# Two projection groups side by side at the start of a hybrid decoder block, and one set of copies moved to ScalarE

## The chip, the cores and the metric

The kernel runs on one core of a Trainium2 chip. Its metric is the device time of one execution in microseconds. A core has five engines with an instruction queue each: TensorE (PE, with its weight loads as PEld) multiplies matrices into PSUM banks; VectorE (DVE), ScalarE (ACT) and GpSimd (POOL) do elementwise work; SyncE (SP) mostly issues DMAs. An engine takes its own instructions in program order, and waits at one until the semaphores of the tiles it reads and writes allow it.

## What is computed

S = 512 positions, D = 1024, one layer, float32:

```python
h = rms_norm(x, norm_g)
proj = h @ w_in            # 4 x 512 + 4 x 512 + 2 x 1024 + 8 columns
fq, fk, fv, fz, mq, mk, mv, mz, ga, gb, fl = split_cols(proj, IN_SPLITS)
q, k = rms_norm(heads(fq)), rms_norm(heads(fk))        # 8 heads of 64
log_f = log_sigmoid(fl + b_f)
y_fox = attention(q, k, heads(fv), bias=cumsum(log_f)) * silu(fz)
q, k = rope(rms_norm(heads(mq))), rope(rms_norm(heads(mk)))
y_moba = block_attention(q, k, heads(mv)) * silu(mz)
merged = (sigmoid(ga + b_gate[0]) * (y_fox @ w_fox)
          + sigmoid(gb + b_gate[1]) * (y_moba @ w_moba))
out = x + merged @ w_out
```

## The kernel before, in words

**Products.** Every float32 operand of a projection is split in two parts of a shorter type, a high part (a rounded copy) and a low part (the rest). A product Z·w is then three matmuls: Zh·wh, Zh·wl, Zl·wh. Activations stand transposed, 1024 rows in KT = 8 slices k of 128, 512 positions each. The projection's columns are worked off in groups of 256: fqa, fka, fza, fzb, fva, then fqb, fkb, fvb, the eight m groups, wf0 to wf3 (the product with w_fox), the gate groups GA and GB, wm and wo. A group of the q, k or v kind has four units, one for each 128 positions, 24 matmuls into one PSUM bank each. A z group and a wf group have two units, transposed (L402, L403), of 512 columns.

**Weights.** A weight group arrives as one or two raw tiles of 128 x 4 x 256 (tag "wr", four buffers); `split` (L131 to L137) has ScalarE copy it to wh (L134) and VectorE subtract to get wl. `pump` issues loads ahead as buffers come free.

**The normalisation.** The first four groups do not wait for the RMS norm. `split_x` (L121 to L126) makes Zh, Zl from the raw rows of x times the norm's gain (ScalarE's product L125, VectorE's subtraction L126), and fqa, fka, fza, fzb multiply these; the factor 1/rms comes in later. `x_stats` (L218 to L229) loads x once more, in eight tiles, has ScalarE square and sum each (L225), and VectorE and GpSimd make mm and r of the sums (from L226). `norm_row` (L234 to L238) spreads r over the partitions (p_rbc, rbc), and `normalise` (L240 to L244) makes the normalised Gh and Gl, eight slices, which fva and all later groups use.

**The start.** `first_loads` (L65 to L86) issues the DMAs of the rows xt0 to xt7 and of fqa's weights on SyncE's queue, the first four slices in small pieces (k=0, k=1, k=2 and 3), the constants cs on ScalarE's queue. TensorE first runs WARM = 8 matmuls on zeros (L107). `first_split` (L148 to L160) splits fqa's weights piece by piece, with the split of the rows between; then wfl (the eight forget columns) and fka's two raw tiles are loaded whole, in `load_fl` (L139 to L146, tag "qk"). `first_qk` (L371 to L382) multiplies fqa, all eight k for its four banks, and after it fka, 264 columns wide because it carries the forget columns. fqa has its banks in "pj" and "lg", fka its in "tp" and "pv". Then come, in the program: x_stats, the evacuation of the eight banks (`evac_qk`: ScalarE's copy qn L310, for fka VectorE's xf; `norm_qk` per pair of banks: ScalarE's square L324, VectorE's reduction, GpSimd's power L331 and product L333), `forget_exp` (L444), `norm_row`, fza and fzb with `normalise` between, `forget` (L452 to L490: a chain of small VectorE operations on fg, pre, then p_c and p_LR on TensorE, c4), and fva, whose `evac_v` (L335 to L341) has a copy by ScalarE and a subtraction by VectorE (L341).

**The wf products.** `unit_f` (L680 to L691) multiplies a unit of wf into a "pj" bank and has VectorE copy it to FS (L690). The units of wf0 to wf2 run among the last attention group's steps, those of wf3 after it; mzb, just ahead, uses the same banks (evacuated at L422).

**What sets the order.** The program text gives dependences and buffers; a scheduler then orders the instructions of every engine with a timeline of its own, and this order is fixed when the kernel is built. Buffers: "pj" two PSUM banks, "lg" two, "tp" three, "pv" one; raw weights four, wh and wl four each, "qk" four, "y" (rows of x and many others) fifteen. The main sequence stands in L909 to L983.

Of the kernel before, what the change touches and what calls it, by code (L numbers as in the profile page):

```python
# [19 lines left out]
CW = 256  # L20
EPS = 1e-6
NEG = -3.0e38
WARM = 8
WR = 4

C_NG, C_BG, C_FQ, C_FK, C_MQ, C_MK, C_BF, C_GQ, C_GK, C_END = 0, 8, 24, 25, 26, 27, 28, 36, 52, 68
# [3 lines left out]
def fox_moba_kernel(ctx: ExitStack, tc, xT, x, w_in, w_fl, w_fox, w_moba, w_out, cst, rope, out):  # L30


    nc = tc.nc
    V, A, G, T = nc.vector, nc.scalar, nc.gpsimd, nc.tensor

    con = ctx.enter_context(tc.tile_pool(name="con", bufs=1))
    sb = ctx.enter_context(tc.tile_pool(name="sb", bufs=1))
# [3 lines left out]
    stage = {}  # L41
# [7 lines left out]
    def t2(tag, bufs, name, shape=(P, 512), dt=F32):  # L49
        pool = stage["pool"] if tag in ("qs", "pt", "pc", "ys") else sb  # L50
        return pool.tile(list(shape), dt, name=name, tag=tag, bufs=bufs)

    def pst(tag, bufs, name):
        return ps.tile([P, 512], F32, name=name, tag=tag, bufs=bufs)

    def pj(name):
        return pst("pj", 2, name)
# [2 lines left out]
        return pst("tp", 3, name)  # L60


    XT, RAW = {}, {}

    def first_loads():  # L65
        def xt(eng, k):
            XT[k] = t2("y", 15, f"xt{k}")
            eng.dma_start(out=XT[k], in_=xT[:, k, :])

        def w(k0, k1):  # L70
            hf = k0 // 4
            if hf not in RAW:
                RAW[hf] = sb.tile([P, 4, CW], F32, name=f"wr_fqa{hf}", tag="wr", bufs=WR)
            nc.sync.dma_start(out=RAW[hf][:, k0 - 4 * hf:k1 - 4 * hf], in_=w_in[0, :, k0:k1, :])
        nc.scalar.dma_start(out=cs, in_=cst)
        w(0, 1)
        xt(nc.sync, 0)
        w(1, 2)
        xt(nc.sync, 1)
        w(2, 4)  # L80
        xt(nc.sync, 2)
        xt(nc.sync, 3)
        w(4, 8)
        for k in range(4, KT):
            xt(nc.sync, k)


    cs = con.tile([P, C_END], F32, name="cs")
# [1 line left out]
    wfl = con.tile([P, KT, 8], F32, name="wfl")  # L90
    def col(c, n=1):
        return cs[:, c:c + n]
# [12 lines left out]
    wps = pst("tp", 3, "warm_ps")  # L105
    for i in range(WARM):
        T.matmul(wps, warm[:, :P], warm, start=True, stop=True)  # L107
# [10 lines left out]
    Gl = con.tile([P, KT, S], F32R, name="Gl")  # L118
    Z = {}

    def split_x(*ks):  # L121
        for k in ks:
            xt = XT[k]
            zh, zl = Z[k] = [stage["pool"].tile([P, S], F32R, name=f"Z{hl}{k}") for hl in "hl"]
            A.activation(zh, xt, AF.Copy, scale=col(C_NG + k))  # L125
            V.scalar_tensor_tensor(zl, xt, col(C_NG + k), zh.bitcast(F32), op0=OP.mult, op1=OP.subtract)  # L126


    chunks = {}

    def split(src, n, name, half=False):  # L131
        hi = sb.tile([P, 4, 264], F32R, name=f"wh_{name}", tag="wh", bufs=4)
        lo = sb.tile([P, 4, 264], F32R, name=f"wl_{name}", tag="wl", bufs=4)
        A.activation(hi[:, :, 0:n], src, AF.Copy)  # L134
# [4 lines left out]
    def load_fl(name, c0, hf):  # L139
        raw = sb.tile([P, 4, CW], F32, name=f"wr_{name}{hf}", tag="qk", bufs=4)  # L140
        nc.sync.dma_start(out=raw, in_=w_in[c0 // CW, :, 4 * hf:4 * hf + 4, :])
        hi, lo = split(raw, CW, f"{name}{hf}")
        f = wfl[:, 4 * hf:4 * hf + 4, :]
        A.activation(hi[:, :, CW:264], f, AF.Copy)
        V.tensor_tensor(out=lo[:, :, CW:264], in0=f, in1=hi[:, :, CW:264].bitcast(F32), op=OP.subtract)
        chunks.setdefault(name, []).append((hi, lo))  # L146

    def first_split(hf, between):  # L148
        raw = RAW[hf]
        hi = sb.tile([P, 4, 264], F32R, name=f"wh_fqa{hf}", tag="wh", bufs=4)  # L150
        lo = sb.tile([P, 4, 264], F32R, name=f"wl_fqa{hf}", tag="wl", bufs=4)
        for q, xs in enumerate(between):
            k = slice(2 * q, 2 * q + 2) if hf else slice(max(q, 2 * q - 2), max(q + 1, 2 * q))
            if hf == 0 and q < 2:
                V.tensor_copy(hi[:, k, :CW], raw[:, k])
            else:
                A.activation(hi[:, k, :CW], raw[:, k], AF.Copy)
            V.tensor_tensor(out=lo[:, k, :CW], in0=raw[:, k], in1=hi[:, k, :CW].bitcast(F32), op=OP.subtract)
            split_x(*xs)
        chunks.setdefault("fqa", []).append((hi, lo))  # L160

    COLS = {}
    off = 0
    for nm in ("fq", "fk", "fv", "fz", "mq", "mk", "mv", "mz"):
        for hfn in ("a", "b"):
            COLS[nm + hfn] = off
            off += CW
    for nm in ("ga", "gb"):
        for i in range(4):
            COLS[f"{nm}{i}"] = off  # L170
            off += CW

# [45 lines left out]
    def x_stats():  # L218
        G.memset(mh, -0.5)
        for t in range(NT):  # L220
            for hf in range(2):
                xt = t2("y", 15, f"x{t}{hf}")
                nc.sync.dma_start(out=xt, in_=x[t * P:(t + 1) * P, hf * 512:(hf + 1) * 512])
                j = t2("u", 4, "junk")
                A.activation(j, xt, AF.Square, accum_out=ms2[:, t, hf:hf + 1])  # L225
        V.tensor_add(mm, ms2[:, :, 0], ms2[:, :, 1])  # L226
        V.tensor_scalar(mm, mm, 1.0 / D, EPS, op0=OP.mult, op1=OP.add)
        V.tensor_scalar(e2, mm, EPS, None, op0=OP.mult)
        G.tensor_tensor(out=r, in0=mm, in1=mh[:, :NT], op=OP.pow)  # L229
# [138 lines left out]
                        in1=tab[:, ts, None, 24:32].to_broadcast([P, 2, 4, 8]), op=OP.mult)  # L368
        G.tensor_tensor(out=qn[:, :, :, 0:16], in0=ra, in1=rb, op=OP.add)

    def first_qk(name, tags):  # L371
        banks = [pst(tg, n, f"{name}_{i}") for i, (tg, n) in enumerate(tags)]
        n = 264 if name == "fka" else CW
        for kk in range(KT):
            hi, lo = chunks[name][kk // 4]
            k = kk % 4
            for t in range(NT):
                st = slice(t * P, (t + 1) * P)
                T.matmul(banks[t][:, :n], Z[kk][0][:, st], hi[:, k, :n], start=(kk == 0), stop=False)
                T.matmul(banks[t][:, :n], Z[kk][0][:, st], lo[:, k, :n], start=False, stop=False)  # L380
                T.matmul(banks[t][:, :n], Z[kk][1][:, st], hi[:, k, :n], start=False, stop=(kk == KT - 1))
        return banks  # L382

    def unit(name, t):
        def go():
# [283 lines left out]
    FS, MG = {}, {}  # L669

    def br_mm(p, name, br, c):
        hi, lo = chunks[name][0]
        cc = slice(c * P, (c + 1) * P)
        for k in range(4):
            yh, yl = Y[br, k]
            T.matmul(p, hi[:, k, cc], yh, start=(k == 0), stop=False)  # L676
            T.matmul(p, hi[:, k, cc], yl, start=False, stop=False)  # L677
            T.matmul(p, lo[:, k, cc], yh, start=False, stop=(k == 3))  # L678

    def unit_f(i, c):  # L680
        def go():
            j = 2 * i + c
            p = pj(f"pf{j}")
            br_mm(p, f"wf{i}", "f", c)
            if j == 0:
                f = sb.tile([P, 4, S], F32, name="f03", tag="v", bufs=2)
                FS[0], FS[1] = f[:, 0:2, :], f[:, 2:4, :]
            elif j in (4, 6):
                FS[j // 2] = sb.tile([P, 2, S], F32, name=f"f{j}", tag="qk", bufs=4)
            V.tensor_copy(FS[i][:, c, :], p)  # L690
        return go  # L691

    SG = {}
# [9 lines left out]
    def group(name):  # L703
# [213 lines left out]
    for t in range(NT):  # L917
        evac_qk(b1[t], "fqa", t)
# [5 lines left out]
    fz = filler(["fza", "fzb"])  # L924
# [119 lines left out]
```

## Time and profile before

| | |
|---|---|
| median of 3 runs | 433.29 us (433.22 to 433.48) |
| the profiled execution | 432.65 us |
| its span, first to last instruction | 430.9 us |
| instructions | 8095 |
| granted TensorE clock, mean | 1.00 |
| GpSimd's busy time | 86.6 us (20%) |
| moved by DMA | 56.13 MB, 130 GB/s on the mean |
| moved in the first 10.8 us, in the next two such slices | 245, 398, 293 GB/s |

Times of the trace are microseconds from the span's start. A row of the timeline has a start, a duration from first to last instruction of the row, the engine, the line, the operation, what is written and read, the shape, the count, and in brackets how long the engine stood idle before it and what ended that. SPq is SyncE's queue of DMA issues. A row of the groups has the count, the shortest, median and longest duration in ns, and the times of the first and the last.

### The profile page before, as it was taken

Reading aid. Unit: us, or ns where it says so; the run is one execution under the profiler, and the core shown is the slowest. Engines: PE = TensorE matmul, PEld = TensorE weight load, DVE = VectorE, ACT = ScalarE, POOL = GpSimd, SP = SyncE. Lnnn points to the kernel's source line nnn. Section 1 sums busy time; section 2 is a strip of 40 time slices with the busy share of each in tenths; the row PEclk is TensorE's granted clock in tenths of the full one; section 3 lists DMA queues with packets and bytes.
Section 4 is the critical chain, followed back from the end, with each engine's and each line's share of the span. In section 5 each row is a group of like instructions: output and inputs, shape, how many; then the busy total and the mean of one; then the engine's idle time right before and its main releaser. Section 6 shows DMA issues by size and latency. Waiting matters only on the chain.

```text
span 430.9 us, 8095 instructions
## 1 busy us (share of the span) xinstructions
PE 424.5 (99%) x3103; PEld 400.5 (93%) x3103; DVE 313.7 (73%) x559; ACT 249.6 (58%) x480; POOL 86.6 (20%) x108
## 2 busy tenths in 40 slices
PE   8999999999999999999999999999999999999996
PEld 6998899999999998999998878899999989999996
DVE  5679965869979867767856898959897796673311
ACT  4986336876868767677765855547655545531100
POOL 1049200227044660044630003020000000000000
PEclk9999999999999999999999999999999999999999
DMA  7981235326565413303304305561415306525221
GB/s 245 398 293 54 94 102 152 98 79 206 170 213 176 140 39 119 122 13 122 111 15 137 110 13 186 181 196 52 146 50 184 110 3 211 187 96 166 85 92 46
DMA packets 25670, 56.13 MB, mean 130 GB/s; under 512 B 3240, under 2 KB 11872, under 8 KB 25632
## 3 DMA queue, kind: packets, MB, share of 16 engines
q1 hardware_dynamic: 14528, 40.08, 28.0%
q10 hardware_dynamic: 9952, 11.34, 8.8%
q0 software_dynamic: 1152, 4.19, 2.7%
q8 instruction: 24, 0.39, 0.4%
q14 instruction: 14, 0.11, 0.1%
HBM read 46.01 MB, written 6.32 MB: 121 GB/s over the span
## 4 chain that ended last, share of the span: by engine, by line
PE 96%; DVE 2%; DMA 1%; issue 0%; SPq 0%; DVEq 0%
PE pb_GB L750 3%; PE pb_GA L750 3%; PE pb_GB L749 3%; PE pb_GA L747 3%; PE pb_GB L747 3%; PE pb_GA L749 3%; PE po L847 3%; PE po L849 3%; PE po L848 3%; PE pv L608 2%; PE pv L607 2%; PE lg L553 2%; PE lg L552 2%; PE pm L676 2%; PE pm L677 2%; PE pm L678 2%
## 5 line engine op out<-in xcount | busy, mean ns | idle before, releaser
L557 ACT ACTIVATE p<-p,negm 128x128 f32<-128x128 f32 (+1 forms) x64 | 35.7, 558 | 14.4 <-DVE negm L555 12.2
L331 POOL TENSOR_TENSOR ff<-ss,mh 128x8 f32<-128x8 f32 x16 | 27.8, 1743 | 65.5 <-DVE ss L329 65.1
L555 DVE CUSTOM_DVE_ANT_0 p<-lg,mask 128x128 f32<-128x128 f32 (+1 forms) x64 | 30.8, 485 | 13.0 <-PE lg L553 12.3
L847 PE MATMUL po<-wh_wo,mgh 128*128 128x256 f32 x96 | 27.1, 282 | 0.0
L849 PE MATMUL po<-wh_wo,mgl 128*128 128x256 f32 x96 | 27.0, 282 | 0.0
L848 PE MATMUL po<-wl_wo,mgh 128*128 128x256 f32 x96 | 26.9, 281 | 0.0
L857 DVE TENSOR_TENSOR ot<-po,xr 128x256 f32<-128x256 f32 x16 | 6.6, 424 | 24.7 <-PE po L849 23.5
L134 ACT ACTIVATE wh_wo<-wr_wo 128x1024 fp32r<-128x1024 f32 x8 | 8.5, 1061 | 21.6 <-PE po L849 8.0
L552 PE MATMUL lg<-KH,QS 128*128 128x128 f32 (+1 forms) x64 | 20.5, 329 | 0.0
L633 DVE TENSOR_TENSOR ypair<-pv,ysh 64x512 f32<-64x512 f32 x16 | 11.0, 687 | 12.9 <-ACT ysh L632 12.8
L136 DVE TENSOR_TENSOR wl_GB<-wr_gb,wh_GB 128x1024 fp32r<-128x1024 f32 x14 | 16.8, 1224 | 4.2 <-ACT wh_GB L134 3.3
L136 DVE TENSOR_TENSOR wl_GA<-wr_ga,wh_GA 128x1024 fp32r<-128x1024 f32 x14 | 17.9, 1294 | 2.5 <-ACT wh_GA L134 2.4
L134 ACT ACTIVATE wh_GB<-wr_gb 128x1024 fp32r<-128x1024 f32 x14 | 14.6, 1059 | 8.6 <-PE pm L677 2.5
L134 ACT ACTIVATE wh_GA<-wr_ga 128x1024 fp32r<-128x1024 f32 x14 | 14.6, 1059 | 8.5 <-PE pb_GA L749 4.3
L848 PEld LDWEIGHTS po<-wl_wo,mgh 128*128 128x128 f32 x96 | 18.1, 189 | 0.0
L849 PEld LDWEIGHTS po<-wh_wo,mgl 128*128 128x128 f32 x96 | 18.1, 189 | 0.0
L847 PEld LDWEIGHTS po<-wh_wo,mgh 128*128 128x128 f32 x96 | 18.1, 189 | 0.0
L136 DVE TENSOR_TENSOR wl_wo<-wr_wo,wh_wo 128x1024 fp32r<-128x1024 f32 x8 | 9.8, 1222 | 7.4 <-ACT wh_wo L134 7.4
L632 ACT ACTIVATE ysh<-pv 64x512 f32<-64x512 f32 x16 | 9.5, 594 | 8.9 <-PE pv L608 6.4
L604 DVE TENSOR_TENSOR ptl<-p_a,pth 128x512 fp32r<-128x512 f32 x16 | 11.0, 686 | 4.1 <-ACT pth L603 4.1
L676 PE MATMUL pf<-yhf,wh_wf 128*128 128x512 f32 x32 | 13.2, 414 | 0.6 <-DVE zs_mzb L422 0.6
L526 DVE SCALAR_TENSOR_TENSOR QS<-p_qT,cs,QS 64x512 fp32r<-64x512 f32 x16 | 12.0, 750 | 2.5 <-ACT QS L525 2.2
(447 smaller groups left out, 1769.9 us busy)
## 6 DMA issues: line engine op xcount, KB each, us to landing
wr_ga<-in_w_in_dram SPq DMA_DIRECT2D x8, 512.0 KB, 3.5
wr_gb<-in_w_in_dram SPq DMA_DIRECT2D x8, 512.0 KB, 5.0
wr_wo<-in_w_out_dram SPq DMA_DIRECT2D x8, 512.0 KB, 4.2
xt<-in_xT_dram SPq DMA_DIRECT2D x8, 256.0 KB
x<-in_x_dram SPq DMA_DIRECT2D x8, 256.0 KB, 7.2
KH<-KH ACTq DMA_DIRECT2D x16, 128.0 KB, 2.4
s_dramh<-sum_sh ACTq DMA_DIRECT2D x8, 256.0 KB
s_draml<-sum_sl ACTq DMA_DIRECT2D x8, 256.0 KB, 4.4
```

Source lines behind the costliest of these rows:

```text
L134: A.activation(hi[:, :, 0:n], src, AF.Copy)
L136: eng.tensor_tensor(out=lo[:, q, 0:n], in0=src[:, q], in1=hi[:, q, 0:n].bitcast(F32), op=OP.subtract)
L331: G.tensor_tensor(out=f2, in0=ss.rearrange("p t h -> p (t h)"), in1=mh, op=OP.pow)
L552: T.matmul(lg[:, :n], qs[:, qt], kh[:, :n], start=True, stop=False)
L555: V.tensor_tensor_reduce(pt, lg[:, :n], mask[:, 512 - n:512], -0.125, 3.0e38, op0=OP.add, op1=OP.min, accum_out=mkn[:, hh, i:i + 1])
L557: A.activation(pt, pt, AF.Exp, bias=mkn[:, hh, i:i + 1], scale=-1.0, accum_out=rs[:, hh, i:i + 1])
L747: T.matmul(o, hi[:, k, cc], lh, start=(n < 3 and c == 0 and k == 0), stop=False, skip_group_check=True)
L749: T.matmul(o, hi[:, k, cc], ll, start=False, stop=False, skip_group_check=True)
L750: T.matmul(o, lo[:, k, cc], lh, start=False, stop=(k == 3), skip_group_check=True)
L847: T.matmul(p[:, :CW], gh[:, st], hi[:, k, :CW], start=(kk == 0), stop=False)
L848: T.matmul(p[:, :CW], gh[:, st], lo[:, k, :CW], start=False, stop=False)
L849: T.matmul(p[:, :CW], gl[:, st], hi[:, k, :CW], start=False, stop=(kk == KT - 1))
```

## The change

Two parts. **The start:** fqa and fka are multiplied side by side, slice by slice: for each k first fqa's twelve products, then fka's. For that fka's weights are loaded in the same small pieces as fqa's, between the rows of x, and the first rows xt0 come in two halves of 256 positions, each split by itself. wfl goes to ScalarE's queue, right behind cs, and its split to the first use of each half of fka. Only the first piece of weights is rounded by VectorE (before, the first two). WARM is 6. `load_fl` goes; `COLS` only moves up. **The wf products:** ScalarE, not VectorE, copies the eight banks out.

```diff
-WARM = 8
+WARM = 6
...
     def first_loads():
-        def xt(eng, k):
-            XT[k] = t2("y", 15, f"xt{k}")
-            eng.dma_start(out=XT[k], in_=xT[:, k, :])
-
-        def w(k0, k1):
+        def w(nm, k0, k1):
             hf = k0 // 4
...
+            if (nm, hf) not in RAW:
+                tag, bufs = ("wr", WR) if nm == "fqa" else ("qk", 4)
+                RAW[nm, hf] = sb.tile([P, 4, CW], F32, name=f"wr_{nm}{hf}", tag=tag, bufs=bufs)
+            nc.sync.dma_start(out=RAW[nm, hf][:, k0 - 4 * hf:k1 - 4 * hf],
+                              in_=w_in[0 if nm == "fqa" else COLS["fka"] // CW, :, k0:k1, :])
+
+        def xt(k, c0=0, c1=S):
+            if k not in XT:
+                XT[k] = t2("y", 15, f"xt{k}")
+            nc.sync.dma_start(out=XT[k][:, c0:c1], in_=xT[:, k, c0:c1])
         nc.scalar.dma_start(out=cs, in_=cst)
-        w(0, 1)
-        xt(nc.sync, 0)
-        w(1, 2)
-        xt(nc.sync, 1)
-        w(2, 4)
-        xt(nc.sync, 2)
-        xt(nc.sync, 3)
-        w(4, 8)
-        for k in range(4, KT):
-            xt(nc.sync, k)
+        nc.scalar.dma_start(out=wfl, in_=w_fl)
+        w("fqa", 0, 1)
+        xt(0, 0, 256)
+        xt(0, 256, S)
+        w("fka", 0, 1)
+        w("fqa", 1, 2)
+        xt(1)
+        w("fka", 1, 2)
+        w("fqa", 2, 4)
+        xt(2)
+        w("fka", 2, 4)
+        xt(3)
+        w("fqa", 4, 8)
+        xt(4)
+        w("fka", 4, 8)
+        for k in range(5, KT):
+            xt(k)
...
-    def split_x(*ks):
...
+    def split_x(k, parts=1):
+        xt = XT[k]
+        Z[k] = [stage["pool"].tile([P, S], F32R, name=f"Z{hl}{k}") for hl in "hl"]
+        n = S // parts
+        for c in (slice(i * n, (i + 1) * n) for i in range(parts)):
+            zh, zl = (z[:, c] for z in Z[k])
+            A.activation(zh, xt[:, c], AF.Copy, scale=col(C_NG + k))
+            V.scalar_tensor_tensor(zl, xt[:, c], col(C_NG + k), zh.bitcast(F32), op0=OP.mult, op1=OP.subtract)
...
+    def first_split(nm, k0, k1, on_v=False):
+        hf = k0 // 4
+        if len(chunks.setdefault(nm, [])) == hf:
+            hi = sb.tile([P, 4, 264], F32R, name=f"wh_{nm}{hf}", tag="wh", bufs=4)
+            lo = sb.tile([P, 4, 264], F32R, name=f"wl_{nm}{hf}", tag="wl", bufs=4)
+            chunks[nm].append((hi, lo))
+            if nm == "fka":
+                f = wfl[:, 4 * hf:4 * hf + 4, :]
+                A.activation(hi[:, :, CW:264], f, AF.Copy)
+                V.tensor_tensor(out=lo[:, :, CW:264], in0=f, in1=hi[:, :, CW:264].bitcast(F32), op=OP.subtract)
+        hi, lo = chunks[nm][hf]
+        k = slice(k0 - 4 * hf, k1 - 4 * hf)
+        raw = RAW[nm, hf]
+        if on_v:
+            V.tensor_copy(hi[:, k, :CW], raw[:, k])
+        else:
+            A.activation(hi[:, k, :CW], raw[:, k], AF.Copy)
+        V.tensor_tensor(out=lo[:, k, :CW], in0=raw[:, k], in1=hi[:, k, :CW].bitcast(F32), op=OP.subtract)
...
-    def first_qk(name, tags):
...
+    def first_qk(banks, kk):
+        for name, bank in banks.items():
+            n = 264 if name == "fka" else CW
...
             for t in range(NT):
...
-            V.tensor_copy(FS[i][:, c, :], p)
+            A.activation(FS[i][:, c, :], p, AF.Copy)
...
-    first_split(0, ((0,), (1, 2), (3, 4)))
-    first_split(1, ((5, 6), (7,)))
-    nc.sync.dma_start(out=wfl, in_=w_fl)
-    load_fl("fka", COLS["fka"], 0)
-    load_fl("fka", COLS["fka"], 1)
-    b1 = first_qk("fqa", (("pj", 2), ("pj", 2), ("lg", 2), ("lg", 2)))
-    b2 = first_qk("fka", (("tp", 3), ("tp", 3), ("tp", 3), ("pv", 1)))
+    banks = {nm: [pst(tg, n, f"{nm}_{i}") for i, (tg, n) in enumerate(tags)] for nm, tags in
+             (("fqa", (("pj", 2), ("pj", 2), ("lg", 2), ("lg", 2))), ("fka", (("tp", 3), ("tp", 3), ("tp", 3), ("pv", 1))))}
+    for k0, k1 in ((0, 1), (1, 2), (2, 4), (4, 8)):
+        first_split("fqa", k0, k1, k0 == 0)
+        for k in range(k0, k1):
+            split_x(k, 2 if k == 0 else 1)
+            if k == k0:
+                first_split("fka", k0, k1)
+            first_qk(banks, k)
+    b1, b2 = banks["fqa"], banks["fka"]
     x_stats()
```

More of the change, by code (lines that the diff above doesn't have):

```diff
@@ L60, in tp @@
         return pst("tp", 3, name)
+    COLS = {}
+    off = 0
+    for nm in ("fq", "fk", "fv", "fz", "mq", "mk", "mv", "mz"):
+        for hfn in ("a", "b"):
+            COLS[nm + hfn] = off
+            off += CW
+    for nm in ("ga", "gb"):
+        for i in range(4):
+            COLS[f"{nm}{i}"] = off
+            off += CW
     XT, RAW = {}, {}
     def first_loads():
-        def xt(eng, k):
-            XT[k] = t2("y", 15, f"xt{k}")
-            eng.dma_start(out=XT[k], in_=xT[:, k, :])
-        def w(k0, k1):
+        def w(nm, k0, k1):
             hf = k0 // 4
-            if hf not in RAW:
-                RAW[hf] = sb.tile([P, 4, CW], F32, name=f"wr_fqa{hf}", tag="wr", bufs=WR)
-            nc.sync.dma_start(out=RAW[hf][:, k0 - 4 * hf:k1 - 4 * hf], in_=w_in[0, :, k0:k1, :])
-        nc.scalar.dma_start(out=cs, in_=cst)
-        w(0, 1)
-        xt(nc.sync, 0)
-        w(1, 2)
-        xt(nc.sync, 1)
-        w(2, 4)
-        xt(nc.sync, 2)
-        xt(nc.sync, 3)
-        w(4, 8)
-        for k in range(4, KT):
-            xt(nc.sync, k)
+            if (nm, hf) not in RAW:
[7 more added lines that the diff above has]
+            nc.sync.dma_start(out=XT[k][:, c0:c1], in_=xT[:, k, c0:c1])
+        nc.scalar.dma_start(out=cs, in_=cst)
+        nc.scalar.dma_start(out=wfl, in_=w_fl)
[15 more added lines that the diff above has]
+            xt(k)
     cs = con.tile([P, C_END], F32, name="cs")
@@ L119, in fox_moba_kernel @@
     Z = {}
-    def split_x(*ks):
[L122 to L126, printed above, removed]
+    def split_x(k, parts=1):
[6 more added lines that the diff above has]
+            V.scalar_tensor_tensor(zl, xt[:, c], col(C_NG + k), zh.bitcast(F32), op0=OP.mult, op1=OP.subtract)
     chunks = {}
@@ L137, in split @@
         return hi, lo
[L139 to L171, printed above, removed]
+    def first_split(nm, k0, k1, on_v=False):
[16 more added lines that the diff above has]
+        V.tensor_tensor(out=lo[:, k, :CW], in0=raw[:, k], in1=hi[:, k, :CW].bitcast(F32), op=OP.subtract)
@@ L369, in do_rope @@
         G.tensor_tensor(out=qn[:, :, :, 0:16], in0=ra, in1=rb, op=OP.add)
-    def first_qk(name, tags):
-        banks = [pst(tg, n, f"{name}_{i}") for i, (tg, n) in enumerate(tags)]
-        n = 264 if name == "fka" else CW
-        for kk in range(KT):
+    def first_qk(banks, kk):
+        for name, bank in banks.items():
+            n = 264 if name == "fka" else CW
             hi, lo = chunks[name][kk // 4]
@@ L378, in first_qk @@
                 st = slice(t * P, (t + 1) * P)
[L379 to L382, printed above, removed]
+                T.matmul(bank[t][:, :n], Z[kk][0][:, st], hi[:, k, :n], start=(kk == 0), stop=False)
+                T.matmul(bank[t][:, :n], Z[kk][0][:, st], lo[:, k, :n], start=False, stop=False)
+                T.matmul(bank[t][:, :n], Z[kk][1][:, st], hi[:, k, :n], start=False, stop=(kk == KT - 1))
     def unit(name, t):
```

## The prediction

> **What bounds the kernel now.** I began with the engines' busy shares and the chain of work that ended last.
>
> ```profile
> PE 424.5 (99%) x3103; PEld 400.5 (93%) x3103; DVE 313.7 (73%) x559; ACT 249.6 (58%) x480; POOL 86.6 (20%) x108
> PE 96%; DVE 2%; DMA 1%; issue 0%; SPq 0%; DVEq 0%
> ```
>
> TensorE is busy for 424.5 of 430.9 us and carries 96% of the chain. An edit can win only where TensorE now idles, and it loses wherever TensorE has to wait for something new. So the next view is busy time by stretch (after the times: the stretch's length, then PE, PEld, DVE, ACT, POOL).
>
> ```profile
> 0.00:5.27 5.27, 3.72 (x8) 2.51 (x8) 1.28 (x5) 2.21 (x3) 1.70 (x10) 1.00 0.56 136
> 5.27:12.27 7.00, 6.62 (x50) 5.98 (x49) 5.40 (x9) 4.57 (x8) 0.00 (x0) 1.00 1.01 362
> 28.70:54.00 25.30, 25.30 (x124) 20.96 (x124) 25.04 (x49) 14.21 (x26) 16.65 (x17) 1.00 0.30 99
> 54.00:100.00 46.00, 45.98 (x381) 45.33 (x380) 33.00 (x79) 30.14 (x67) 8.46 (x6) 1.00 0.36 107
> ```
>
> Two things stand here. Real projection work begins at 5.27 us and has small holes until 12.27, while DMA is saturated. And from 28.7 to 54, where the first groups are evacuated and normalised, **VectorE is full too**: 25.04 of 25.30 us. The change acts on the first, and I ask what it does to the second.
>
> The timeline of TensorE gives the anchors: warm-up, first product, last of fqa and first of fka, first of fza.
>
> ```profile
> 1.55 3.78 PE L107 MATMUL warm_ps<-warm 128*128 128x512 f32 x8 [1.55 <-DVE fg_pre L468]
> 5.27 0.39 PE L379 MATMUL fqa<-wh_fqa,Zh 128*128 128x256 f32 x1
> 17.92 0.28 PE L381 MATMUL fqa<-wh_fqa,Zl 128*128 128x256 f32 x1
> 18.04 0.53 PE L379 MATMUL fka<-wh_fka,Zh 128*128 128x264 f32 x3
> 29.73 0.39 PE L402 MATMUL pz_fza<-Zh,wh_fza 128*128 128x512 f32 x1
> 29.96 0.39 PE L403 MATMUL pz_fza<-Zl,wh_fza 128*128 128x512 f32 x1
> ```
>
> The 96 products of fka run without a hole: 11.69 us, 0.122 each. 17.69 to 18.04 shows fqa's dense pitch, about 0.117; 96 of these are 11.2, but fqa takes 12.77. **1.5 us of holes is all that side-by-side work can fill**, beside an earlier first product.
>
> **The change, part by part. The first stage.** The loads set its pace; these are the first users of each piece.
>
> ```profile
> 0.80 0.38 SPq L74 DMA_DIRECT2D wr_fqa<-in_w_in_dram  x1
> 1.24 0.41 SPq L68 DMA_DIRECT2D xt<-in_xT_dram  x1
> 2.17 0.43 SPq L68 DMA_DIRECT2D xt<-in_xT_dram  x1
> 3.52 0.30 DVE L155 CAST wh_fqa<-wr_fqa 128x256 fp32r<-128x256 f32 x1 [2.01 <-DMA wr_fqa<-in_w_in_dram]
> 4.50 0.72 ACT L125 ACTIVATE Zh<-xt,cs 128x512 fp32r<-128x512 f32 x1 [1.75 <-DMA xt<-in_xT_dram]
> 5.39 0.29 DVE L155 CAST wh_fqa<-wr_fqa 128x256 fp32r<-128x256 f32 x1 [1.12 <-DMA wr_fqa<-in_w_in_dram]
> 6.80 0.72 ACT L125 ACTIVATE Zh<-xt,cs 128x512 fp32r<-128x512 f32 x1 [1.58 <-DMA xt<-in_xT_dram]
> ```
>
> *First product.* A 128 KB piece of weights took 2.72 us from issue to use (0.80 to 3.52), a 256 KB one 3.26. The half piece of xt0 is issued at 1.24, so it is there between 3.96 and 4.50; I take 4.15. Its half-width split costs between 0.29 (the 128x256 cast) and 0.72; I take 0.42. First product at 4.6, bounds 4.3 to 5.0. The six warm-up products end by 1.55 + 6 x 0.43 (3.78 us for eight, less the tail of the last) = 4.1, so they don't block it.
>
> *Step k=0.* 12 x 0.117 + 12 x 0.122 = 2.87 us. Those before about 5.3 run at the warm-up's pace (0.43 for 512 columns against 0.23 at 29.73): some four of them, 0.1 each, so 0.4. TensorE could start k=1 at 4.6 + 2.87 + 0.4 = 7.9.
>
> *Step k=1* needs xt1, now the sixth SP issue and not the fourth. Counted in bytes (896 KB against 768 KB) it lands 0.5 us after the 6.80 of before, at 7.3. Counted in pieces it is later: before, landings followed each other by 0.98, 0.89 and 1.41 us, and the 128 KB piece took as long as its larger neighbour; five steps of about 1.0 after 3.52 give 8.5. I take 7.65, between them. With its 0.72 split and a handoff, k=1 starts at 8.4. Afterwards a step asks for 512 KB in 2.87 us, half of the 362 GB/s above, so nothing else waits. wfl's issue, now second on ScalarE's queue, holds up only the table load (0.4 us, done long before 4.15).
>
> The end of fka, E, is 8.4 + 7 x 2.87 = **28.5 instead of 29.73: 1.2 us early**. Bounds 27.9 (7.9 holds) and 29.4 (by pieces).
>
> **What waits behind it.** Before, fqa's banks were copied out under fka's products. Now fqa ends 12 products before fka does, and ScalarE takes its work in program order. The changed program's order there is: four qn_fqa copies, the split of fzb's first half, two qn_fka copies, and only then the square of the last x tile, from which all of VectorE's chain hangs (mm, r, rbc, the normalisation). Before:
>
> ```profile
> 25.36 1.06 ACT L134 ACTIVATE wh_fzb<-wr_fzb 128x1024 fp32r<-128x1024 f32 x1 [0.24 <-DMA wr_fzb<-in_w_in_dram]
> 27.46 0.63 ACT L225 ACTIVATE junk<-x 128x512 f32<-128x512 f32 x1 [1.03 <-DMA x<-in_x_dram]
> 29.13 1.19 ACT L310 ACTIVATE qn_fka<-fka 128x256 f32<-128x256 f32 x4
> 30.21 1.05 ACT L134 ACTIVATE wh_fzb<-wr_fzb 128x1024 fp32r<-128x1024 f32 x1
> 31.16 1.14 ACT L324 ACTIVATE sq<-qn_fka 128x512 f32<-128x512 f32 x2
> 28.21 0.16 DVE L226 TENSOR_TENSOR mm<-ms 128x4 f32<-128x4 f32 x1 [0.53 <-ACT junk L225]
> ```
>
> There the square starts as its tile lands, 27.46, and VectorE's chain at 28.21, 0.75 later. In the changed kernel fqa's last product ends at E - 12 x 0.122 - 0.117 + 0.28 = E - 1.3. Then, on ScalarE: one copy 0.33, the fzb split 0.95 (30.21 to 31.16), two copies 0.60, the square and handoff 0.75. The chain starts at **E + 1.35 = 29.85, 1.6 us later than before**, though TensorE is earlier.
>
> Its end is VectorE's evacuation of the first fva bank, for which the third fva unit (pj, two banks) waits.
>
> ```profile
> 43.69 0.18 DVE L463 SCALAR_TENSOR_TENSOR fg<-fg,fg 128x32 f32<-128x32 f32 x1
> 57.10 0.11 DVE L481 MEMSET c<- 128x64 f32 x1
> 57.84 0.42 DVE L341 TENSOR_TENSOR v_fva<-pj_fva,v_fva 128x256 fp32r<-128x256 f32 x1
> 58.01 0.28 PE L305 MATMUL pj_fva<-wh_fva,Gl 128*128 128x256 f32 x1
> 58.31 0.39 PE L303 MATMUL pj_fva<-wh_fva,Gh 128*128 128x256 f32 x1
> ```
>
> Before, it ends at 58.26 and TensorE goes on at 58.31, 0.18 later than its pitch from 58.01 asks: the two were level. From 28.21 to 58.31 are 30.1 us, and VectorE is full all the way. The changed order has the same instructions in between, less what stood from 57.10 to 57.84 (0.74) and one more fg step (0.1), plus a wait of about 0.15 for the exp that now follows the reduces: 29.4. So the third fva unit starts at E + 1.35 + 29.4 = E + 30.75 = 59.25, **0.95 us later than 58.31**. TensorE by itself would be there at E + 28.4 (from fza's start to the end of the second fva unit before, 29.73 to 58.13): it stalls 2.3 us. The early gain is spent and more.
>
> After that VectorE has slack (33.0 of 46 us from 54 to 100), and TensorE's order is that of before from the group mqb on, so I carry 0.95 to the end.
>
> **The wf products.** Eight copies go from VectorE to ScalarE.
>
> ```profile
> L690 DVE COPY f<-pf x8: 669/682/692, 249.1 to 278.6; 128x512 f32<-128x512 f32 x8
> 35.27 0.60 ACT L238 ACTIVATE rbc<-p_rbc 128x512 f32<-128x512 f32 x1 [2.85 <-PE p_rbc L237]
> 250.00:260.00 10.00, 10.00 (x51) 8.25 (x50) 9.39 (x18) 4.83 (x13) 0.00 (x0) 1.00 0.11 31
> PE pf L676 <- DVE zs_mzb L422: 0.6, 2, 0.4
> ```
>
> VectorE loses 8 x 0.68 = 5.4 us where it is nearly full, ScalarE gets 8 x 0.60 where it is half idle. But TensorE has no hole from 250 to 260; the 0.6 us it waits for pf's bank is for mzb's evacuation, which stands ahead of the first copy in both orders. Bounds: gain 0.6, loss 0.6 (one copy in front of a KH split). I take 0.
>
> **Sum.** -1.2 at fka's end, +2.15 given back at the third fva unit, 0 for wf: +0.95. The profiled execution took 432.65 us (span 430.9), 0.64 below the median 433.29; I put the difference on the median: **434.3 us**, with E's bounds 433.7 to 435.2.
>
> **Rivals.** *The clock is released late (slower).* Before, the quick pitch set in only after a burst without a pause from 1.55 to 5.27; the granted clock reads 1.00 throughout and doesn't show it, the pitch does. With six warm-ups TensorE pauses from 4.1 to 4.6. If another such spell (3.7 us) counts from 4.6, products run at about 0.215 until 8.3: 17 of the 24, the rest ends at 9.15, E is 29.25 and the time 435.0. Against it: the pause is short.
> [...]
>
> *VectorE's chain does not bind (faster).* Three rows of that chain are long:
>
> ```profile
> 34.24 0.83 DVE L459 TENSOR_TENSOR fg<-fg,fg 128x32 f32<-128x32 f32 x1
> 35.11 0.97 DVE L460 TENSOR_TENSOR fg<-fg 128x32 f32<-128x32 f32 x1
> 33.98 2.04 POOL L333 TENSOR_TENSOR qn_fqa<-qn_fqa,ff 128x512 f32<-128x512 f32 x2
> L242 DVE SCALAR_TENSOR_TENSOR xt<-xt,cs,rbc x8: 740/747/1536, 36.8 to 43.0; 128x512 f32<-128x512 f32 x8
> ```
>
> Their neighbours of that size take 0.18, and one normalisation 1.54 against 0.75; GpSimd's products run beside the first two. If GpSimd's work moves off them, 0.65 + 0.8 + 0.8 = 2.25 us goes, the stall with it, and TensorE keeps its 1.2 to 1.5: 431.9. It decides from 2.3 us on. Against: GpSimd's work hangs from the same start, so I expect it to move along.
>
> *Even.* The chain comes out 0.6 to 1 us shorter than my sum (handoffs, two of the three long rows): 433.3.
>
> **How the numbers follow.** Forecast 0.50; late clock 0.12; chain not binding 0.20; even 0.18. A difference of 0.2% (0.87 us) is about what a measurement of this kernel tells from none. Below 432.4 lies the unbound chain: 0.20. Within 0.2% lie the even case and the lower third of the forecast: 0.35. Above 434.2 lies the rest: 0.45. The range takes in most of the unbound chain's case and leaves out some 0.05 below and 0.1 above (half of the late clock, and E at its upper bound): 431.7 to 435.4.
>
> **What would show it.** First product near 4.6; xt1's split between 7.3 and 8.5; fza near 28.5; the square of the last x tile 1.3 us after its tile could have been squared, with VectorE's mm near 29.85; and a hole of about 2 us in TensorE ahead of the third fva unit, whose releaser is VectorE's v_fva. No such hole, or a quick pitch only from 8 us on, would prove me wrong.

## The result, and the profile after

| | before | after |
|---|---|---|
| median | 433.25 us (6 runs, 432.73 to 433.48) | 437.28 us (6 runs, 435.81 to 438.42) |
| ratio, 95% interval | | 1.0094, 1.0081 to 1.0106 |
| the profiled execution, its span | 432.65, 430.9 us | 435.81, 434.1 us |
| last product of TensorE ends | 427.26 us | 430.18 us |

The changed kernel is 4.0 us slower. The forecast was 434.3 in a range of 431.7 to 435.4: the sign was right, the size was not.

I read the changed kernel in the same order. Busy time by stretch (times, length, then PE, PEld, DVE, ACT, POOL, clock, DMA share, GB/s):

```profile
5.27:12.27 7.00, 7.00 (x52) 6.88 (x52) 4.41 (x10) 3.73 (x8) 0.00 (x0) 1.00 0.91 291
28.70:54.00 25.30, 25.30 (x124) 20.98 (x124) 24.36 (x48) 16.13 (x28) 17.52 (x20) 1.00 0.34 118
54.00:100.00 46.00, 44.38 (x368) 43.71 (x367) 32.74 (x78) 26.17 (x58) 5.36 (x4) 1.00 0.35 106
100.00:150.00 50.00, 48.35 (x393) 47.14 (x392) 44.98 (x93) 37.09 (x81) 25.03 (x19) 1.00 0.56 169
```

The side-by-side stage does fill its holes: TensorE is busy for 7.00 of 7.00 us where it was for 6.62. But only 52 products fall into this stretch in place of 50, since its first 1.9 us run at about half the pitch (0.21 us from one product to the next, 6.71 to 6.92, where 8.01 to 8.13 is 0.12; see the clock, below). And 1.6 us are lost between 54 and 100, and **1.65 us between 100 and 150, where the kernel before was full** (50.00). The list of TensorE's waits (what it waited for, total, times, longest) names them:

```profile
PE pj_fva L312 <- DVE v_fva L350: 1.6, 1, 1.6
PE lg L559 <- DMA KH<-KH: 0.8, 1, 0.8
PE pj_mqa L312 <- DVE v_fvb L350: 0.8, 1, 0.8
PE pf L683 <- DVE zs_mzb L429: 0.4, 1, 0.4
```

The timeline of the same kernel, the rows that answer to the steps of the forecast:

```profile
4.83 0.58 PE L387 MATMUL fqa<-wh_fqa,Zh 128*128 128x256 f32 x1 [0.36 <-ACT Zh L148]
6.71 0.41 PE L387 MATMUL fqa<-wh_fqa,Zh 128*128 128x256 f32 x1
6.92 0.41 PE L388 MATMUL fqa<-wl_fqa,Zh 128*128 128x256 f32 x1
8.01 0.28 PE L389 MATMUL fka<-wh_fka,Zl 128*128 128x264 f32 x1
8.13 0.28 PE L388 MATMUL fka<-wl_fka,Zh 128*128 128x264 f32 x1
8.92 0.39 PE L387 MATMUL fqa<-wh_fqa,Zh 128*128 128x256 f32 x1
29.12 0.39 PE L409 MATMUL pz_fza<-Zh,wh_fza 128*128 128x512 f32 x1
29.64 0.64 ACT L234 ACTIVATE junk<-x 128x512 f32<-128x512 f32 x1
30.40 0.20 DVE L235 TENSOR_TENSOR mm<-ms 128x4 f32<-128x4 f32 x1
58.84 0.41 DVE L350 TENSOR_TENSOR v_fva<-pj_fva,v_fva 128x256 fp32r<-128x256 f32 x1
59.30 0.38 PE L312 MATMUL pj_fva<-wh_fva,Gh 128*128 128x256 f32 x1 [1.62 <-DVE v_fva L350]
113.99 0.35 PE L312 MATMUL pj_mqa<-wh_mqa,Gh 128*128 128x256 f32 x1 [0.82 <-DVE v_fvb L350]
120.96 0.33 PE L559 MATMUL lg<-KH,QS 128*128 128x128 f32 x1 [0.83 <-DMA KH<-KH]
```

fza starts at 29.12, 0.61 early. The third fva unit starts at 59.30, 0.99 late, as forecast (0.95). Then come two holes that were not forecast, 0.82 and 0.83 us of idle time; measured from start to start, with the overlap that is lost ahead of them, each costs about 1 us. The first product of wf stands behind the same work in both kernels, so it shows the sum so far. A second wait for its bank is in the kernel before alone. The first two rows are of that kernel, the third is of the changed one:

```profile
244.19 0.50 PE L676 MATMUL pf<-yhf,wh_wf 128*128 128x512 f32 x1 [0.38 <-DVE zs_mzb L422]
249.22 0.50 PE L676 MATMUL pf<-yhf,wh_wf 128*128 128x512 f32 x1 [0.24 <-DVE zs_mzb L422]
247.51 0.50 PE L683 MATMUL pf<-yhf,wh_wf 128*128 128x512 f32 x1 [0.37 <-DVE zs_mzb L429]
```

At wf the changed kernel is 247.51 - 244.19 = 3.32 us behind: 0.99 from the third fva unit, some 2.0 from the two holes, and 0.3 in pieces too small to name. It wins 0.40 back at that bank, and TensorE's last product ends 430.18 - 427.26 = 2.92 us later. The median is another 1.5 us above this execution.

### The profile page after: what moved, and what is told of

Same layout as the page of the kernel before. It is cut to its first block, busy times and chain, and to the rows that moved or that the text cites. A ratio compares the mean times of both kernels' runs of the same rounds, so it can differ in the third digit from the quotient of the medians.

```text
span 434.1 us, 8088 instructions
## 1 busy us (share of the span) xinstructions
PE 424.4 (98%) x3101; PEld 400.6 (92%) x3101; DVE 310.4 (72%) x552; ACT 253.9 (58%) x491; POOL 91.7 (21%) x108
## 4 chain that ended last, share of the span: by engine, by line
PE 70%; DVE 2%; DMA 1%; ACT 1%; issue 0%; DVEq 0%
PE pb_GB L757 3%; PE pb_GA L757 3%; PE pb_GA L754 3%; PE pb_GB L756 3%; PE pb_GB L754 3%; PE pb_GA L756 3%; PE po L854 3%; PE po L856 3%; PE po L855 3%; PE pv L615 2%; PE pv L614 2%; PE pm L683 2%; PE pm L684 2%; PE pm L685 2%; PE lg L559 2%; PE lg L560 2%
## 5 line engine op out<-in xcount | busy, mean ns | idle before, releaser
L340 POOL TENSOR_TENSOR ff<-ss,mh 128x8 f32<-128x8 f32 x16 | 26.9, 1685 | 74.8 <-DVE ss L338 74.3
L757 PE MATMUL pb_GA<-Gh,wl_GA 128*128 128x256 f32 x48 | 13.6, 283 | 0.0
```

The costliest lines, as they stand in the source:

```text
L340: G.tensor_tensor(out=f2, in0=ss.rearrange("p t h -> p (t h)"), in1=mh, op=OP.pow)
L757: T.matmul(o, lo[:, k, cc], lh, start=False, stop=(k == 3), skip_group_check=True)
```

## The experiments

Three of the questions need an order held still. The scheduler redraws the order of all engines when anything changes in the start; so in several kernels the order that it gave to a donor kernel is imposed from a point on, by edges that fix the order of issue alone and make no instruction wait for another's end (shortened):

```python
for e, idx in ORDER.items():            # the donor's order, by engine
    mine = [i for i in nc.cur_bb.bb.instructions[_m0:] if str(i.engine).split(".")[-1] == e]
    for a, b in zip(idx, idx[1:]):
        tc.add_manual_dep(mine[b], mine[a].name, NoSync, reason="order")
```

### Where the loss sits: wf, order, start

*The wf copies alone,* in the kernel before:

```diff
-            V.tensor_copy(FS[i][:, c, :], p)
+            A.activation(FS[i][:, c, :], p, AF.Copy)
```

> The kernel before with only the second part of the change: ScalarE copies the wf banks. Theory A (the start and the order it leads to carry the whole loss): no change, 433.3 within 0.5, and TensorE's wait for pf stays at about 0.6 us. Rival B (the copies carry part of it): 434 to 435, with new holes of TensorE between 249 and 285 us.

Measured: 432.67 us (before, beside it: 433.44), ratio 0.9985, 0.9976 to 0.9994. A small gain of 0.77, more than either theory gave. TensorE's waits there:

```profile
PE pj_fva L303 <- DVE v_fva L341: 0.5, 1, 0.5
PE pf L676 <- DVE zs_mzb L422: 0.4, 1, 0.4
```

The second wait for pf is gone (0.6 in two before), so the wf copies carry none of the loss. The traces don't show the whole 0.77, though. In the two profiled executions TensorE's last product ends at 427.26 both times: the new order has a hole of 0.46 us ahead of the third fva unit, and the 0.4 us that it costs are what the bank of pf gives back. The rest of the gain is in the medians alone.

*The order alone:* the kernel before up to the attention stage, and from there the order of the changed kernel (of its first part).

> The kernel before, its start and its VectorE copies of wf untouched; but from the attention stage on every engine's instructions are held in the order that the scheduler gave the changed kernel (its first part alone). Theory A (a new order of the attention groups costs the two holes at 113.2 and 120.1 us, 0.95 us each): 435.1, between 434.5 and 435.8, with holes ahead of pj_mqa and lg near 111 and 118 us. Rival B (the holes come because the work arrives late after the start, whatever its order): 433.3 within 0.5 and no such hole.

Measured: 435.07 us, ratio 1.0036, 1.0023 to 1.0049: **1.6 us of loss without any change in the start**, as theory A has it, rival B is out. Of the two holes that theory A expected only the one ahead of lg is there; the timeline shows it with the transfers issued before it:

```profile
113.88 2.13 SPq L204 DMA_DIRECT2D wr_mza<-in_w_in_dram  x2
114.70 0.49 ACTq L529 DMA_DIRECT2D KH<-KH  x1
120.47 0.47 PE L552 MATMUL lg<-KH,QS 128*128 128x128 f32 x1 [2.34 <-DMA KH<-KH]
```

*The start alone,* VectorE's copies of wf, held from the attention on in the order of before:

> The changed start with VectorE's copies of wf; from the attention stage on every engine is held in the order of the kernel before. Theory A: the hole ahead of the third fva unit stays (1.6 us), the holes at 113.2 and 120.1 go: 435.4 (437.3 less 1.9), between 434.2 and 435.8. Rival B (lateness makes the holes): 437.3, the holes near 113 and 120 stay.

Measured: 435.42 us, ratio 1.0050, 1.0032 to 1.0068; the holes near 113 and 120 are gone. But the list of waits shows that the imposed order brought one of its own, ahead of p_LR, since what comes just before the attention is not the donor's:

```profile
PE pj_fva L312 <- DVE v_fva L350: 1.6, 1, 1.6
PE p_LR L496 <- DVE c L493: 1.2, 1, 1.2
```

So this number, though it agrees with theory A's, holds 1.2 us that are not the changed kernel's.

*The first part alone,* no order imposed:

> The first part of the change alone, with VectorE's copies of wf and no order imposed. If the parts add up: 437.2 + 0.8 = 438.0, with the fva hole of 1.6 us and the holes near 113 and 120 us as in the changed kernel. If the wf copies give nothing behind this start: 437.2.

Measured: 437.79 us (4 runs, 434.79 to 439.92), ratio 1.0101, 1.0042 to 1.0159; fva hole 1.6, lg hole 1.4 us, none ahead of pj_mqa. Four executions over 5 us can't tell 438.0 from 437.2: whether the parts add up stays open.

*Any new order?* The kernel before with WARM = 6 has other orders too:

> The kernel before with WARM = 6 and nothing else; it also gets another order of the attention groups from the scheduler. Theory A (a new order is a new draw): the start is as before (first fza near 29.7), but holes appear or go between 60 and 250 us, and the time moves by more than 0.5 us either way: outside 432.9 to 433.9. Rival N (the order of before is as good as others): 433.4 within 0.4, no new hole.

Measured: 433.55 us, ratio 1.0005, 0.9996 to 1.0015, no new hole in the attention groups, as rival N has it. Theory A falls in this general form: a new order isn't a loss by itself, that one was.

### What is wrong with that order

*The order alone, with mza's loads one step later* in SyncE's queue:

> As the start of before with the changed kernel's order, but SyncE issues the two loads of mza (1 MB) one step later, behind the next small copy of LR. Theory K (the copy KH to KH, which the first lg of the next heads waits for 3.4 us after its issue, shares the DMA engines with this load, and so lands late): the hole ahead of lg near 118 us shrinks from 2.34 to under 0.5, the granted clock does not drop after it, 433.2 to 433.8. Rival L (the order puts that lg too close behind its copy, whatever else moves): the hole stays above 1.5 us, 435.1.

Measured: 433.57 us, ratio 1.0011, 1.0001 to 1.0022. The hole of 2.34 us is gone; the longest new wait is

```profile
PE p_ri L577 <- DVE KL L530: 0.3, 1, 0.3
```

Theory K holds. In the order of before the next lg comes 10.5 us after this copy of KH is issued (116.11 to 126.57). The new order puts it 25 mqa products and one pv behind the issue (114.70), where TensorE is ready for it 3.4 us later; and 1 MB of weights is issued 0.8 us before the copy (from 116.94 to 120.35 the DMA share is 0.99, at 300 GB/s). Nothing but these two loads was moved, from 113.88 to 129.73, and with the same lg just as close behind its copy the hole is gone.

*The changed kernel with the same repair,* in its own order:

> The changed kernel in its own order, but the two loads of mza one step later, as was tried behind the start of before. Theory K (that copy's hole, and the clock's drop behind it, are the second half of the loss): no hole ahead of lg near 120 us, no execution with a mean clock of 0.996 or less, 437.2 - 0.95 - 0.85 = 435.4, between 434.6 and 436.0. Rival L (the drops come from the fva hole): executions at 0.996 stay, 436.3 or more.

Measured: 435.65 us (4 runs, 434.60 to 437.04), ratio 1.0060, 1.0036 to 1.0084, in place of 437.2. The lg hole is gone, and 1.5 us with it in the medians, though with four executions the two intervals overlap. One of the four, the profiled one, shows a mean clock of 0.994; its drop comes right behind the fva hole, 2.4 us here. So on the drops rival L was right. That leads to the clock.

### The clock

*The changed kernel once more:*

> The changed kernel once more, for the point at which TensorE's pitch doubles. [...] Rival D (the 0.36 us pause after the warm-up delays the grant): 7.2 again within 0.2, and fza at 29.1.

Measured: 437.14 us (10 runs, 434.44 to 438.80), ratio 1.0080, 1.0056 to 1.0103. In the timeline of its profiled execution the matmuls come twice as fast from 5.8 on, not from 7.2:

```profile
5.36 0.41 PE L387 MATMUL fqa<-wh_fqa,Zh 128*128 128x256 f32 x1
5.57 0.39 PE L388 MATMUL fqa<-wl_fqa,Zh 128*128 128x256 f32 x1
6.04 0.28 PE L387 MATMUL fqa<-wh_fqa,Zh 128*128 128x256 f32 x1
6.16 0.28 PE L388 MATMUL fqa<-wl_fqa,Zh 128*128 128x256 f32 x1
28.69 0.39 PE L409 MATMUL pz_fza<-Zh,wh_fza 128*128 128x512 f32 x1
```

Same program, nearly the same pause (0.29 and 0.36 us), and a point 1.4 us earlier: rival D is out. The kernel before has the quick pitch from 5.27. The forecast's rival of a late clock is half right: its cause, the pause, doesn't stand, but the quick pitch did come late. From one execution of the same program to the next it moved from 7.20 to 5.8, and the side-by-side start pays for it (fza at 29.12 against 28.69); what sets the point wasn't shown.

Of the 16 executions of the changed kernel that were timed, nine show a mean clock of 0.998 or more and lie between 434.4 and 437.5 us; seven show 0.990 to 0.996, and lie between 436.8 and 438.8. 0.4% of 437 us are 1.75 us, one stretch of 3.41 us at half clock; the medians of the two sets, 436.4 and 438.2, are as far apart. Of more than a hundred executions of the kernel before with a clock on record one falls under 0.998 (0.994, 434.23 us). A mean of 0.998 stands for some 1.7 us at half clock (2 x 0.002 x 433, an estimate). That much can lie at the end alone, where TensorE has stopped: its last product ends 3.6 us before the span does in the kernel before (427.26 of 430.9), and in the changed kernel's profile the stretch from 430.60 to 434.00, without a product, reads 0.98. Where the drop sits shows in the windows of two kernels, first the one with the order alone, cut at the steps of the clock:

```profile
116.94:120.35 3.41, 1.19 (x10) 0.88 (x8) 3.28 (x6) 1.56 (x4) 0.00 (x0) 1.00 0.99 300
120.36:123.77 3.41, 3.30 (x14) 3.02 (x15) 2.20 (x8) 1.64 (x5) 0.00 (x0) 0.50 0.83 268
123.78:127.19 3.41, 3.41 (x31) 3.41 (x30) 2.62 (x8) 2.86 (x9) 0.47 (x1) 1.00 0.22 49
```

then the whole change with the last x tile first (held from forget on, see below), whose only long hole is the one ahead of the third fva unit,

```profile
56.41:59.81 3.40, 1.66 (x14) 1.46 (x13) 3.33 (x11) 0.38 (x1) 0.00 (x0) 1.00 0.36 93
59.83:63.22 3.39, 3.39 (x18) 3.39 (x17) 0.78 (x5) 0.00 (x0) 0.00 (x0) 0.50 0.64 213
```

and, for the other side, the changed kernel's second profile, whose clock held, cut around its hole:

```profile
57.02:60.41 3.39, 1.71 (x14) 1.51 (x14) 3.32 (x11) 0.68 (x2) 0.00 (x0) 1.00 0.76 234
60.43:63.84 3.41, 3.41 (x32) 3.41 (x30) 1.43 (x7) 0.66 (x2) 0.00 (x0) 1.00 0.18 72
```

**In these profiles each stretch of 3.4 us at half clock stands right behind 3.4 us in which TensorE was busy for less than half** (matmuls x18 in place of x31 where the hole was that of fva): behind 1.19 of 3.41 us, 1.66 of 3.40, and 1.44 of 3.40 in the changed kernel with the later mza loads; behind 1.71 of 3.39 the clock held. So 1.74 us of idle time in such a stretch (3.40 - 1.66) went with a drop, 1.68 (3.39 - 1.71) did not. A hole's length alone doesn't tell: in the kernel with the square first and the wf copies (below) TensorE waits 2.6 us at fza, in an execution with a mean clock of 1.000. Four stretches are too few for a limit, and what decides wasn't shown; a hole of about 1.7 us, as the changed kernel has, came with a drop in one profile and without one in another. Where the clock drops, the hole costs some 1.7 us more (half of 3.4, an estimate). In the changed kernel itself the drops are read from the mean clock alone: both of its profiled executions held.

### The hole ahead of the third fva unit

The forecast blamed ScalarE's order, which squares the last x tile behind the copies of fqa. *The square first* (on the start held in the old order):

```diff
+    with tc.issue_after(last_on(mybir.EngineType.Activation)):
         for t in range(NT):
             evac_qk(b1[t], "fqa", t)
...
```

> As the start with the old order (changed start, VectorE's copies of wf, order of before from the attention on), but ScalarE takes the square of the last x tile ahead of all copies of fqa and fka. Theory S (the late start of VectorE's chain makes both holes, 1.62 us ahead of the third fva unit and 1.19 us ahead of p_LR): VectorE's mm starts near 29.0 in place of 30.43 (by the bytes of the queue the tile lands about 28.2), the first hole shrinks to 0.3 and the second goes, 435.4 - 1.3 - 1.2 = 432.9, between 432.4 and 433.6. Rival G (the chain is as long as its contention with GpSimd makes it, or the tile lands late anyway): 435.4, both holes stay above 1 us.

> As the kernel with the square first, but with ScalarE's copies of wf, and from the attention on the order of the kernel that has this part alone. Both theories: 0.6 to 0.8 us less than the kernel with the square first, as the wf copies gave by themselves; by theory S 432.2, faster than the kernel before; by rival G 434.7.

Measured: 436.46 us (ratio 1.0076, 1.0059 to 1.0093) and 436.67 us (1.0093, 1.0057 to 1.0129). Theory S falls as a repair: mm starts at 30.02, only 0.4 earlier than the 30.43 of the held start (29.0 was expected), v_fva comes later and not earlier (59.48 against 58.87), the p_LR hole stays (1.3 us), and TensorE now waits at fza as well, whose bank is freed by the copies that were put back. In the second of the two the tile itself came late:

```profile
30.31 0.63 ACT L234 ACTIVATE junk<-x 128x512 f32<-128x512 f32 x1 [1.04 <-DMA x<-in_x_dram]
...
PE pz_fza L409 <- ACT qn_fqa L319: 2.6, 1, 2.6
PE pj_fva L312 <- DVE v_fva L350: 1.3, 1, 1.3
```

*The last x tile earlier in SyncE's queue,* ahead of the 2 MB for fza and fzb:

```diff
     x_stats()
+    x31 = last_on(mybir.EngineType.SP)
...
     norm_row()
-    pump(0)
+    with tc.issue_after(x31):
+        pump(0)
```

> The changed start with VectorE's copies of wf and, from the attention on, the order of before; but SyncE issues the last tile of x ahead of the four loads of fza and fzb (2 MB), not behind them. Theory Q (VectorE's chain starts late because that tile lands late in the queue, at about 29.1 in place of 27.46, and not because of ScalarE's order): mm starts before 26 us, both holes (1.62 us ahead of the third fva unit, 1.19 us ahead of p_LR) go, 435.4 - 2.8 = 432.6, between 432.1 and 433.3. Rival G (the chain is as long as before from fka's end on, since xf and the norm of fka wait for fka anyway): the holes stay above 1 us, 435.4.

> As the kernel with the last x tile first, but with ScalarE's copies of wf and the order of the kernel that has these alone. Both theories: 0.7 us less than with the last x tile first alone; by theory Q 431.9, which would be faster than both kernels; by rival G 434.7.

> The changed kernel with the last x tile issued ahead of the loads of fza and fzb, and no order imposed. By theory Q the fva hole (1.6 us) goes here too; what the scheduler then makes of the attention groups is another draw: 435.4 if the holes near 113 and 120 us stay, 432 to 433.5 if they do not. By rival G 437.2 with the fva hole above 1 us.

Measured: 434.97 us (1.0037, 1.0025 to 1.0049), 433.84 us (1.0012, 1.0001 to 1.0024) and 435.92 us (1.0053, 1.0034 to 1.0072). The timeline of the first and its waits:

```profile
23.90 0.63 ACT L234 ACTIVATE junk<-x 128x512 f32<-128x512 f32 x1
24.65 0.16 DVE L235 TENSOR_TENSOR mm<-ms 128x4 f32<-128x4 f32 x1 [4.29 <-ACT junk L234]
57.42 0.41 DVE L350 TENSOR_TENSOR v_fva<-pj_fva,v_fva 128x256 fp32r<-128x256 f32 x1
...
PE p_LR L496 <- DVE c L493: 1.2, 1, 1.2
```

The chain starts 5.75 us earlier and v_fva comes 1.4 us earlier (57.42 against 58.84); the fva hole is down to 0.03 us. Theory Q is right for this hole; the one ahead of p_LR stays, in the second kernel too (1.2 us). In the third kernel, with the scheduler's own order, mm starts as early (25.57), and the hole is 1.4 all the same. So the late tile is only a part of the cause: the other part is where v_fva stands in VectorE's order. One more, the whole change with that tile first, and held from forget on:

> The whole change, with the last x tile issued ahead of the loads of fza and fzb, and from forget on (not only from the attention on) the order of the kernel that has the wf copies alone, so that the 1.2 us hole ahead of p_LR, which the imposed order brought, goes. Theory H (the loss is the sum of the holes and of the clock): 433.84 less 1.2 = 432.6, between 432.0 and 433.2, level with the kernel that has the wf copies alone (432.67): the start then gives no more than 0.3. Rival I (something else in the changed start costs a us or more over the whole span): 433.8.

Measured: 433.87 us (433.00 to 437.14), ratio 1.0030, 1.0006 to 1.0054. The p_LR hole is gone; but this order has both splits of fqb just ahead of v_fva, which again comes at 58.71:

```profile
57.38 1.22 DVE L159 TENSOR_TENSOR wl_fqb<-wr_fqb,wh_fqb 128x1024 fp32r<-128x1024 f32 x1
58.71 0.41 DVE L350 TENSOR_TENSOR v_fva<-pj_fva,v_fva 128x256 fp32r<-128x256 f32 x1
...
PE pj_fva L312 <- DVE v_fva L350: 1.7, 1, 1.7
```

So this run decides nothing between theory H and rival I. Four of its ten executions lost a stretch of the clock (0.994 and 0.995, 434.9 to 437.1 us); the five at 0.999 and more took 433.0 to 433.5.

### What is left of the start without its holes

*The whole change, tile first, VectorE's copies for p_LR ahead of fkb:*

> The whole change, the last x tile ahead of the loads of fza and fzb, the order of the kernel with the wf copies alone from the attention on, and VectorE's copies for p_LR ahead of its work for fkb. Theory H (holes and the clock's drops behind them are the whole loss): the kernel with the last x tile first and the wf copies had one hole of 0.39 us ahead of the third fva unit and one of 1.20 ahead of p_LR; the second goes, no execution drops its clock: 433.84 - 1.2 = 432.6, between 432.1 and 433.1, and no faster than the old start with the same repair (432.48). Rival I (the side by side start does gain once nothing waits behind it): 431.9 or less. Rival J (the start has a further cost): 433.3 or more.

*The start of before with the wf copies and the tile first:*

> The start of before with ScalarE's copies of wf, and the last x tile issued ahead of the loads of fza and fzb; order of the kernel that has the wf copies alone from forget on. That kernel had a hole of 0.46 us ahead of the third fva unit. Theory Q: it goes, 432.67 - 0.4 = 432.3, the fastest of all. Rival: the 2 MB behind that tile come later, fza's weights with them, and nothing is gained: 432.7 or more.

Measured: 433.25 us (12 runs, 432.08 to 434.71), ratio 0.9999, 0.9987 to 1.0010; and 432.48 us (10 runs, 431.85 to 434.05), ratio 0.9985, 0.9974 to 0.9996. The first kernel's longest waits behind the start:

```profile
PE pj_fva L312 <- DVE v_fva L350: 0.4, 1, 0.4
PE pf L684 <- DVE zs_mzb L429: 0.4, 1, 0.4
PE p_b L605 <- DVE ptl L612: 0.2, 1, 0.2
```

Without its holes the whole change is level with the kernel before, wf copies included. Beside the old start with the tile first and the same copies it is 0.6 us (by the ratios) to 0.8 us (by the medians) behind, and the intervals just overlap. Theory H gave 432.6, rival J 433.3 or more: what takes this last part isn't settled. The two kernels on the old start, with 432.67 and 432.48, are the only ones clearly faster than the kernel before.

## Why the prediction was wrong in size, step by step

- **First product 4.6, k=1 at 8.4, fka's end 28.5.** Measured 4.83, 8.92 and 29.12 (4.77, 8.35 and 28.69 in the second profile); the first product and the end are inside their bounds. What is missing is the clock: half pitch was reckoned until 5.3, and lasted to 7.20 and 5.8.
- **VectorE's chain at E + 1.35.** Measured E + 1.28 (30.40). The reason given, ScalarE's order alone, did not stand: the square put first helped nothing, the tile put first in the queue did. That tile's load is issued at 21.55 in place of 19.66, which the forecast didn't count; so the size agrees in part by luck.
- **Third fva unit at 59.25, a stall of 2.3 us, 0.95 behind.** Measured 59.30, 1.62 idle (1.78 beyond the pitch), 0.99 behind. The early gain is spent at that bank, as forecast, so the rival of a chain that doesn't bind is out. The close hit is luck: E came 0.62 late, and from mm to this product VectorE took 28.9 us in place of 29.4. With the tile first and the order of before behind it, the hole goes to 0.03 us.
- **wf: 0 within 0.6.** Measured a gain of 0.77 by itself, of which the traces show 0.4, at the second wait for pf.
- **The step that failed: "After that VectorE has slack, and TensorE's order is that of before from the group mqb on, so I carry 0.95 to the end."** From mqb on that holds: the changed kernel stays some 3.3 us behind from there to wf. But between the third fva unit and mqb the order is another, which the forecast put at nothing, and there the 0.99 grows to 3.32. One place of that order sets a lg close behind a copy of KH while 1 MB of weights is moving: about 1 us in this profile, 1.6 us in the median by the order alone, gone when the load is moved. The other hole, ahead of pj_mqa, waits for VectorE's v_fvb and costs about 1 us in this profile; it is not in the second one, nor in the kernel with the start alone, and its cause stays open.
- **Left out: that a hole can cost twice.** In the windows above holes of 1.7, 2.3 and 2.4 us were followed by 3.4 us at half clock; by their mean clock seven of 16 executions of the changed kernel have one or two. The forecast knew the late grant as a rival, not the drop.

For the median of 437.28, the start (1.0), the order (1.6 to 1.9) and wf (-0.8) give 435.1 to 435.4 from 433.25. A drop of 1.75 us in about half of the executions is a good part of the rest; but the nine without one have a median of 436.4, so 1.0 to 1.3 us stay open. The lg hole differs from run to run (0.8 and 0.6 us in the two profiles of the changed kernel, 1.4 with the start alone, 2.3 with the order alone), which may be it. In which executions which hole dropped the clock wasn't traced.

## What to carry to other kernels

When a scheduler decides the order, a change in one place is a new order in all places: compare the orders of the whole program, and look in each new one for consumers that have moved up to their transfers. Count a hole of TensorE as a risk: here holes of 1.7, 2.3 and 2.4 us were each followed by 3.4 us at half clock, some 1.7 us more by estimate, and one with 1.68 us of idle time was not. And an early start pays only if what ends last behind it, here one VectorE evacuation at 58 us, is moved along; in these runs it brought nothing even then.

## What the runs showed of the hardware

- The quick pitch of TensorE's products (0.12 us each in place of 0.21) set in at 5.27 us of the span in the kernel before, and at 7.20 and 5.8 in two executions of the changed kernel, with a pause of 0.36 and 0.29 us after the warm-up.
- In three profiles the clock read 0.50 for one stretch of 3.39 to 3.41 us, each right behind a stretch of that length in which TensorE was busy for 35% (1.19 of 3.41), 42% (1.44 of 3.40) and 49% (1.66 of 3.40); behind one of 50% (1.71 of 3.39) it read 1.00.
- A copy of 128 KB from SBUF to SBUF, with a median of 2.4 us over the kernel before, let its lg go only 5.8 us after its issue (114.70 to 120.47) with 1 MB of weights issued 0.8 us ahead of it (113.88), at a DMA share of 0.99 from 116.94 to 120.35.
- Between 5.27 and 12.27 us the loads moved 291 GB/s in the changed kernel, which has more of them in small pieces, at a DMA share of 0.91; before, 362 at 1.01.
